# A hybrid decoder block on one core: where two plain weight loads of a paired projection stand in the load queue

## The chip, the cores and the metric

The kernel runs on one core of a Trainium2 chip. The metric is the device time of one execution in microseconds. Three runs of the kernel before gave 1426.63, 1428.28 and 1429.77 us; the median, 1428.28 us, is the time before. The engines are named as in the profile: PE is TensorE (PEld its weight loads), DVE VectorE, ACT ScalarE, POOL GpSimd, SP SyncE, which here only issues DMAs.

## The reference

One layer on x of shape (1, 256, 2048), float32: RMSNorm, one input projection for q, k, v and three gates, three causal token mixers, a gated merge, an output projection, then RMSNorm and a SwiGLU feed-forward layer of width 5632.

```python
h = rmsnorm(x, g_mix)
proj = h @ w_in                       # 2048 x 12288: q, k, v (16 heads of 128) and 3 gates of 2048
...
merged = (gates[:, :, 0] * (flat(o_a) @ w_branch[:ea])
          + gates[:, :, 1] * (flat(o_b) @ w_branch[ea:eb])
          + gates[:, :, 2] * (flat(o_c) @ w_branch[eb:]))
x = x + merged @ w_out
h2 = rmsnorm(x, g_ffn)
gu = h2 @ w_gu                        # 2048 x 11264: gate and up
x = x + (jax.nn.silu(gu[..., :D_FF]) * gu[..., D_FF:]) @ w_down
```

The attention mixers work on 256 tokens and are small beside the five weight matrices, which are read from HBM once each.

## The kernel before, in words

**Products.** Each float32 operand is split in two float32r parts, a high part (a cast on ACT) and a low part (source minus high part, on DVE): `split`, L109 and L110. A product of two operands is three matmuls (`product`, L162, matmuls at L164 to L166): high by high, low weight by high, high weight by low. A weight piece is 256 rows by 512 columns, 512 KB, in one tile of 128 x 2 x 512. `load` (L282) fetches one, `parts` (L288) splits one into w_hi and w_lo, which have five buffers each.

**Paired projections.** `project_pair` (L325) makes two column blocks A and B of 512 columns at once. Over the first two of the four 512-row chunks of the 2048 rows (`acts.wc`, chunks 0 and 1) it saves one product in eight: each chunk's weights are a 2 x 2 grid of pieces b11, b12, b21, b22 (first index the half of the rows, second the column block), and seven products of sums of pieces with sums of activations replace eight. They are called forms 1 to 7 here, each for both chunks. A `quarter` (L312) is the loading of one grid place for both chunks, two loads, into the pool `gx` under the name g_raw, which has six buffers. The other two chunks are done plainly: `rest` (L340) loads one piece under the name w_raw (four buffers, in `wpool`), splits it and makes twelve matmuls. Per pair there are eight loads of g_raw and eight of w_raw, 22 splits, and 84 + 96 matmuls of 512 columns.

**Banks.** X and Y take a pair of PSUM banks in turn (ps and qs); Z and V are z and v from the gate pairs on. The order of a pair is:

- `begin_pair` (L315), which the pair before runs ahead at its own end: loads b11, b12, splits b11, adds u = b11 + b12, loads b21 and splits it
- form 1 into X, a copy of X (`snapshot`, L303, L305), form 2 into Y, form 5 (with u) into Z, a copy of Z
- b22's two loads
- `rest` for the first two plain pieces of block B, into Z and V
- u += b22 (`add_into`, L308, L310) and form 6 into X, a third plain piece, b12 += b22 and form 7 into X, the fourth plain piece
- sums for the results c22 and c12, form 3 and form 4, four plain pieces of block A, the next pair's `begin_pair`

After it a gate pair scales and stores its results (L672, ACT), a gate/up pair does silu and the product with up (L889 on ACT, L890 on DVE).

**Order.** A scheduler orders the instructions of PE, DVE and ACT by a time model, but weight loads (except those of w_down and of the unpaired projections) are kept in program order on SP's queue by `fetch` (L105). So one queue carries, per pair, b11, b12, b21 (six g_raw), b22 (two g_raw), and the eight w_raw. A load waits on the queue until the buffer it takes has been read by its last readers; what is behind it on the queue waits too. With six buffers of g_raw, the two b22 loads take the buffers of b11, which are free once b11 is split.

**Which pairs there are.** Twenty: four for q and k, five for gates, and eleven for gate and up. In the q/k pairs Z and V are ps and qs too.

Of the kernel before, what the change touches and what calls it, by code (L numbers as in the profile page):

```python
# [57 lines left out]
def hybrid_block(ctx: ExitStack, tc: tile.TileContext, x, w_in, w_branch, w_out, w_gu, w_down, rel_bias, xT, gains,  # L58
# [24 lines left out]
    def pool(stack, name, side, bufs=1):  # L83
        return stack.enter_context(tc.tile_pool(name=name, bufs=bufs, side=side, reuse_waits="tile"))
# [8 lines left out]
    def half_kb(dt=F32):  # L93

        return scratch.tile([P, NB], dt, name="sc")
# [3 lines left out]
    def banks():  # L99

        turn.reverse()
        return [acc.tile([P, NB], F32, name=turn[1]) for _ in range(2)]
# [6 lines left out]
    def split(hi, lo, src, pin=False):  # L109
        for op in nc.scalar.copy(hi, src), nc.vector.tensor_sub(lo, src, hi.bitcast(F32)):  # L110
            if pin:
                tc.keep_in_program_order(op)
# [19 lines left out]
    def advance(queue):  # L132
        while queue:
            try:
                next(queue[0])
                return
            except StopIteration:
                queue.pop(0)
# [23 lines left out]
    def product(ps, ah, al, wh, wl, start=False, stop=False):  # L162
        how = dict(skip_group_check=True)
        nc.tensor.matmul(ps, ah, wh, start=start, stop=False, **how)  # L164
        nc.tensor.matmul(ps, ah, wl, start=False, stop=False, **how)  # L165
        nc.tensor.matmul(ps, al, wh, start=False, stop=stop, **how)  # L166
# [115 lines left out]
    def load(w, k, col0, pl=None):  # L282

        raw = pl.tile([P, 2, NB], F32, name="g_raw", bufs=6 if pl is gx else 4) if pl else wpool.tile([P, 2, NB], F32, name="w_raw", bufs=4)
        (nc.sync.dma_start if w is w_down else fetch)(raw, w[k * P:(k + 2) * P, col0:col0 + NB].rearrange("(k p) n -> p k n", p=P))
        return raw

    def parts(src):  # L288
        hi = wpool.tile([P, 2, NB], F32R, name="w_hi")
        lo = wpool.tile([P, 2, NB], F32R, name="w_lo")  # L290
        split(hi, lo, src)
        advance(stages)
        split_count[0] += 1
        if split_count[0] % 2:
            advance(slow_stages)
        for step in at_split.pop(split_count[0], ()):
            step()
        return hi, lo
# [4 lines left out]
    def snapshot(ps):  # L303
        sb = half_kb()
        nc.scalar.copy(sb, ps)  # L305
        return sb

    def add_into(dsts, srcs):  # L308
        for d, a in zip(dsts, srcs):
            tc.keep_in_program_order(nc.vector.tensor_add(d, d, a))  # L310

    def quarter(acts, w, kh, col0):  # L312
        return [load(w, 4 * c + 2 * kh, col0, gx) for c in acts.wc]

    def begin_pair(acts, w, colA, colB):  # L315

        b11, b12 = (quarter(acts, w, 0, col0) for col0 in (colA, colB))
        p11 = [parts(b) for b in b11]
        u = [gx.tile([P, 2, NB], F32, name="u") for _ in acts.wc]
        for a, b, d in zip(b11, b12, u):  # L320
            nc.vector.tensor_add(d, a, b)  # L321
        b21 = quarter(acts, w, 1, colA)
        return p11, b12, u, b21, [parts(b) for b in b21]

    def project_pair(acts, w, colA, colB, begun=None, nxt=None):  # L325

        cols = (colA, colB)
        X, Y = banks()  # L330
        Z, V = others()

        def form(ps, f, srcs, start, stop, split=False):
            for i, c in enumerate(acts.wc):
                wh, wl = srcs[i] if split else parts(srcs[i])
                for j in range(2):
                    product(ps, *acts.form(f, c, j), wh[:, j], wl[:, j], start and i + j == 0,
                            stop and i + j == len(acts.wc))

        def rest(n, k, p0, p1, start=False, stop=False):  # L340
            wh, wl = parts(load(w, k, cols[n]))
            for t, ps in ((1, p1), (0, p0)):
                for j in range(2):
                    product(ps, *acts.plain(t, k + j), wh[:, j], wl[:, j], bool(start and t == 1 and j == 0), stop and j == 1)

        ks = [k for c in range(KT // 4) if c not in acts.wc for k in (4 * c, 4 * c + 2)]
        p11, b12, u, b21, p21 = begun or begin_pair(acts, w, colA, colB)
        form(X, 1, p11, True, True, True)
        s1 = snapshot(X)
        form(Y, 2, p21, True, False, True)  # L350
        form(Z, 5, u, True, True)
        z5 = snapshot(Z)
        b22 = quarter(acts, w, 1, colB)
        rest(1, ks[0], Z, V, start=True)
        rest(1, ks[1], Z, V)
        add_into(u, b22)
        form(X, 6, u, False, True)
        x2 = snapshot(X)
        rest(1, ks[2], Z, V)
        add_into(b12, b22)  # L360
        form(X, 7, b12, False, True)
        x3 = snapshot(X)
        rest(1, ks[3], Z, V, stop=True)
        nc.vector.tensor_sub(z5, z5, x3)
        c22 = half_kb()
        nc.vector.tensor_add(c22, V, z5)
        form(Z, 3, b22, False, True)
        c12 = half_kb()
        nc.vector.tensor_sub(c12, Z, x2)
        for k in ks[:2]:  # L370
            rest(0, k, Y, X)
        add_into(u, b21)
        form(X, 4, u, False, False)
        for k in ks[2:]:
            rest(0, k, Y, X, stop=k == ks[-1])
        ahead = begin_pair(*nxt) if nxt else None
        c11 = half_kb()
        nc.vector.tensor_add(c11, Y, s1)
        return (c11, X, c12, c22), ahead
# [9 lines left out]
    p1 = pool(ph1, "p1", "left")  # L389
# [343 lines left out]
    for (kind, what), after in zip(units, units[1:] + [(None, None)]):  # L733
        if kind == "gates" and what[0] == chunks[4]:
            finish_stages(slow_stages)
            pat.close()
            acc2 = ctx.enter_context(tc.tile_pool(name="acc2", bufs=1, space=PSUM))
            others = beside
            o = Columns(pool(ph1, "o", "left"), "o", NH)
            for i in range(NH // 4):  # L740
                at_split[split_count[0] + 22 * i + 12] = [lambda k=4 * i: split_o(k)]
        nxt = pair_of(*after)
        if kind in ("qk", "gates"):
            ps, ahead = project_pair(*pair_of(kind, what), ahead, nxt)
            if others is in_turn:
                turn.reverse()
        else:
            ps = project(h, 0, w_in, 0, KT, V0 + what * NB if kind == "v" else gate_col(*what),
                         *((ps0, FIRST) if (kind, what) == ("v", 0) else ()))
            ahead = begin_pair(*nxt) if nxt else None  # L750
        finish_stages(stages)
        if kind == "v":
            keep_v(what, ps)
        elif kind == "qk":
            keep_qk(what, *ps)
        elif kind == "gate":
            keep_gate(*what, ps)
        else:
            keep_gate(*what[0], ps[:2])
            keep_gate(*what[1], ps[2:])  # L760
# [123 lines left out]
    for c in range(D_FF // NB):  # L884
        nxt = (h2, w_gu, (c + 1) * NB, D_FF + (c + 1) * NB) if c + 1 < D_FF // NB else None
        (g0, g1_, u0, u1), ahead = project_pair(h2, w_gu, c * NB, D_FF + c * NB, ahead, nxt)
        sg = [half_kb() for _ in range(NT)]
        for t, (g, u) in enumerate(((g0, u0), (g1_, u1))):
            nc.scalar.activation(sg[t], g, AF.Silu, scale=rstd2[:, t:t + 1])  # L889
            nc.vector.scalar_tensor_tensor(sg[t], u, rstd2[:, t:t + 1], sg[t], op0=ALU.mult, op1=ALU.mult)  # L890
        if c < NF // 4 - 2:
            to_a_by_dma(c, sg)
        else:
            stages.append(to_a(c, sg))
# [153 lines left out]
```

## Time and profile before

| | |
|---|---|
| median of three runs | 1428.28 us (1426.63 to 1429.77) |
| the profiled execution | 1427.54 us |
| its span, first to last instruction | 1425.8 us |
| DVE busy, ACT busy | 83%, 64% |
| DMA | 313.76 MB, mean 220 GB/s |
| w_raw loads from w_gu | 88, 512 KB each, 6.3 us from issue to landing (median) |
| g_raw loads from w_gu | 88, 512 KB each, 5.7 us (median) |

The page's first part gives busy time per engine and its share of the span. A group row reads: line, engine, operation, output <- inputs, count, then busy us, mean ns and the idle time of the engine before it with what ended it. In a timeline a row is start, length, engine, line, operation, and in brackets the idle time of that engine before it with its releaser. Rows of the same kind that follow each other are merged ("x2"). PE's matmuls overlap: each is shown with its full length, about 0.39 us, while one starts every 0.23 us, so what PE loses is read from the starts. In the chain of waits a row is start, length and what was under way.

### The profile page before, as it was taken

How to read it: one execution, taken by the hardware profiler on the slowest of the kernel's cores; microseconds unless marked ns; L12 is line 12 of the kernel's file. 1: busy time of each engine (PE TensorE's matmuls, PEld its weight loads, DVE VectorE, ACT ScalarE, POOL GpSimd, SP SyncE). 2: the span in 40 equal slices, each digit the busy share in tenths (PEclk: the TensorE clock that was granted, in tenths of full speed). 3: DMA queues.
4: the chain of work that ended last, by engine and by line, in shares of the span. 5: the costliest groups of instructions: out<-in, count | busy, mean ns of one | idle time of the engine just before them, and what ended most of it. 6: DMA issues, size and time to landing. Idle time of an engine off the chain costs nothing. (4 is left out here: it accounts for less than half of the span.)

```text
span 1425.8 us, 17593 instructions
## 1 busy us (share of the span) xinstructions
PE 1411.4 (99%) x6297; PEld 1159.1 (81%) x6297; DVE 1190.0 (83%) x1265; ACT 909.5 (64%) x1160; POOL 65.1 (5%) x121
## 2 busy tenths in 40 slices
PE   8999999999999999999999999999999999999998
PEld 6888788888888888888888887778888888788887
DVE  7898797867799997876689999999999998886775
ACT  7767777767666665444456677676777776654453
POOL 1000000000000002100100000000000010100000
PEclk9999999999999999999999999999999999999999
DMA  9764547374656757866686667577977786776552
GB/s 331 277 221 135 205 134 247 108 250 162 222 177 236 256 195 276 297 224 213 220 299 221 216 190 233 187 219 244 268 223 218 250 237 228 251 238 235 191 172 94
DMA packets 174056, 313.76 MB, mean 220 GB/s; under 512 B 29800, under 2 KB 32384, under 8 KB 173968
## 3 DMA queue, kind: packets, MB, share of 16 engines
q1 hardware_dynamic: 144672, 277.38, 58.0%
q0 software_dynamic: 8992, 29.45, 5.9%
q10 hardware_dynamic: 20304, 5.80, 2.8%
q8 instruction: 49, 0.80, 0.2%
q14 instruction: 39, 0.32, 0.1%
HBM read 293.17 MB, written 14.70 MB: 216 GB/s over the span
## 5 line engine op out<-in xcount | busy, mean ns | idle before, releaser
L110 DVE TENSOR_TENSOR w_lo<-w_raw,w_hi 128x1024 fp32r<-128x1024 f32 x332 | 403.3, 1221 | 122.4 <-ACT w_hi L110 119.4
L110 ACT CAST w_hi<-w_raw 128x1024 fp32r<-128x1024 f32 x332 | 346.3, 1050 | 171.4 <-PE qs L166 53.4
L110 ACT CAST w_hi<-g_raw 128x1024 fp32r<-128x1024 f32 x184 | 190.8, 1052 | 111.2 <-PE ps L166 31.9
L110 ACT CAST w_hi<-u 128x1024 fp32r<-128x1024 f32 x138 | 145.0, 1053 | 155.5 <-DVE u L310 77.5
L110 DVE TENSOR_TENSOR w_lo<-g_raw,w_hi 128x1024 fp32r<-128x1024 f32 x184 | 219.1, 1220 | 30.0 <-ACT w_hi L110 29.0
L110 DVE TENSOR_TENSOR w_lo<-u,w_hi 128x1024 fp32r<-128x1024 f32 x138 | 164.3, 1220 | 21.4 <-ACT w_hi L110 20.8
L165 PE MATMUL ps<-w_lo,h_hi 128*128 128x512 f32 x352 | 137.9, 392 | 1.2 <-DVE w_lo L110 1.2
L166 PE MATMUL ps<-w_hi,h_lo 128*128 128x512 f32 x352 | 137.3, 390 | 0.0
L164 PE MATMUL ps<-w_hi,h_hi 128*128 128x512 f32 x352 | 131.9, 391 | 0.0
L165 PE MATMUL qs<-w_lo,h_hi 128*128 128x512 f32 x332 | 129.7, 391 | 0.0
L166 PE MATMUL qs<-w_hi,h_lo 128*128 128x512 f32 x332 | 129.2, 390 | 0.0
L164 PE MATMUL qs<-w_hi,h_hi 128*128 128x512 f32 x332 | 122.9, 391 | 0.0
L310 DVE TENSOR_TENSOR u<-u,g_raw 128x1024 f32<-128x1024 f32 x80 | 94.1, 1218 | 0.0
L165 PEld LDWEIGHTS ps<-w_lo,h_hi 128*128 128x128 f32 x352 | 66.1, 188 | 15.5 <-DVE w_lo L110 1.9
L166 PEld LDWEIGHTS ps<-w_hi,h_lo 128*128 128x128 f32 x352 | 66.1, 188 | 13.6
L164 PEld LDWEIGHTS ps<-w_hi,h_hi 128*128 128x128 f32 x352 | 65.9, 188 | 13.3
L166 PEld LDWEIGHTS qs<-w_hi,h_lo 128*128 128x128 f32 x332 | 62.3, 188 | 12.8
L165 PEld LDWEIGHTS qs<-w_lo,h_hi 128*128 128x128 f32 x332 | 62.3, 188 | 12.8
L164 PEld LDWEIGHTS qs<-w_hi,h_hi 128*128 128x128 f32 x332 | 62.3, 188 | 12.7
L321 DVE TENSOR_TENSOR u<-g_raw 128x1024 f32<-128x1024 f32 x40 | 48.7, 1219 | 20.9 <-DMA g_raw<-in_w_in 16.3
L165 PE MATMUL v<-w_lo,h_hi 128*128 128x512 f32 x120 | 48.0, 400 | 2.9 <-DVE w_lo L110 2.7
L310 DVE TENSOR_TENSOR g_raw<-g_raw 128x1024 f32<-128x1024 f32 x40 | 47.1, 1219 | 0.0
(386 smaller groups left out, 2940.8 us busy)
## 6 DMA issues: line engine op xcount, KB each, us to landing
w_raw<-in_w_in SPq DMA_DIRECT2D x116, 512.0 KB, 5.0
g_raw<-in_w_gu SPq DMA_DIRECT2D x88, 512.0 KB, 5.7
w_raw<-in_w_gu SPq DMA_DIRECT2D x88, 512.0 KB, 6.3
g_raw<-in_w_in SPq DMA_DIRECT2D x72, 512.0 KB, 5.4
w_raw<-in_w_down SPq DMA_DIRECT2D x64, 512.0 KB, 4.7
w_raw<-in_w_branch SPq DMA_DIRECT2D x32, 512.0 KB, 5.9
w_raw<-in_w_out SPq DMA_DIRECT2D x32, 512.0 KB, 4.7
g_raw<-in_w_down SPq DMA_DIRECT2D x24, 512.0 KB, 5.3
```

The source lines that it names most:

```text
L110: for op in nc.scalar.copy(hi, src), nc.vector.tensor_sub(lo, src, hi.bitcast(F32)):
L164: nc.tensor.matmul(ps, ah, wh, start=start, stop=False, **how)
L165: nc.tensor.matmul(ps, ah, wl, start=False, stop=False, **how)
L166: nc.tensor.matmul(ps, al, wh, start=False, stop=stop, **how)
L310: tc.keep_in_program_order(nc.vector.tensor_add(d, d, a))
L321: nc.vector.tensor_add(d, a, b)
```

## The change

The first two plain loads of block B are issued before the two loads of b22 in program order, and so on the same queue; their splitting and products stay where they were.

```diff
-        def rest(n, k, p0, p1, start=False, stop=False):
-            wh, wl = parts(load(w, k, cols[n]))
+        def rest(n, k, p0, p1, start=False, stop=False, raw=None):
+            wh, wl = parts(raw or load(w, k, cols[n]))
...
         z5 = snapshot(Z)
+        first = [load(w, k, cols[1]) for k in ks[:2]]
         b22 = quarter(acts, w, 1, colB)
-        rest(1, ks[0], Z, V, start=True)
-        rest(1, ks[1], Z, V)
+        rest(1, ks[0], Z, V, start=True, raw=first[0])
+        rest(1, ks[1], Z, V, raw=first[1])
```

The queue of a pair then carries six g_raw, two w_raw, two g_raw, six w_raw. All twenty pairs run this code. The sizes, the buffers and the number of instructions of each kind stay the same.

## The prediction

> **What bounds the kernel now.** I read the page first, for the engine that carries the span.
>
> ```profile
> PE 1411.4 (99%) x6297; PEld 1159.1 (81%) x6297; DVE 1190.0 (83%) x1265; ACT 909.5 (64%) x1160; POOL 65.1 (5%) x121
> ...
> PEclk9999999999999999999999999999999999999999
> ```
>
> TensorE is busy nearly all the time at full clock, so only its small holes can be won. The next view groups who waited for whom, for the weight loads that run ahead of the matmuls, between 420 and 1080 us. That stretch holds most of the paired projections with their own banks z and v (gates and gate/up weights).
>
> ```profile
> PEld v L165 <- DVE w_lo L110: 6.8, 10, 1.1
> PEld qs L165 <- DVE w_lo L110: 2.0, 4, 0.8
> PEld ps L165 <- DVE w_lo L110: 2.0, 5, 0.5
> ```
>
> Columns: waiter, releaser, us in total, times, longest. Ten times the first product of a plain quarter into v waits for its low part, which VectorE makes from w_raw. To see why that is late I followed one of the ten, the pair around 940 us: the chain of waits, then the timelines of PE, ScalarE and VectorE.
>
> ```profile
> 940.02 6.07 DMA w_raw<-in_w_gu
> ```
>
> ```profile
> 947.73 0.39 PE L166 MATMUL z<-w_hi,h_slo 128*128 128x512 f32 x1
> 947.95 0.39 PE L164 MATMUL v<-w_hi,h_hi 128*128 128x512 f32 x1
> 948.53 0.50 PE L165 MATMUL v<-w_lo,h_hi 128*128 128x512 f32 x1 [0.19 <-DVE w_lo L110]
> 948.87 0.39 PE L166 MATMUL v<-w_hi,h_lo 128*128 128x512 f32 x1
> ```
>
> ```profile
> 940.44 2.19 ACT L110 CAST w_hi<-u 128x1024 fp32r<-128x1024 f32 x2 [2.12 <-PE qs L166]
> 942.54 0.72 ACT L889 ACTIVATE sc<-sc,rstd 128x512 f32<-128x512 f32 x1
> 943.16 0.67 ACT L889 ACTIVATE sc<-qs,rstd 128x512 f32<-128x512 f32 x1
> 943.73 0.57 ACT L305 COPY sc<-ps 128x512 f32<-128x512 f32 x1
> 946.17 1.05 ACT L110 CAST w_hi<-w_raw 128x1024 fp32r<-128x1024 f32 x1 [1.86 <-DMA w_raw<-in_w_gu]
> 947.12 1.35 ACT L860 COPY joined<-turned 128x1024 uint16<-128x1024 uint16 x1
> 948.35 1.03 ACT L110 CAST w_hi<-w_raw 128x1024 fp32r<-128x1024 f32 x1
> ```
>
> ```profile
> 923.42 1.22 DVE L110 TENSOR_TENSOR w_lo<-w_raw,w_hi 128x1024 fp32r<-128x1024 f32 x1
> 925.16 1.22 DVE L110 TENSOR_TENSOR w_lo<-w_raw,w_hi 128x1024 fp32r<-128x1024 f32 x1
> ...
> 937.17 4.63 DVE L110 TENSOR_TENSOR w_lo<-g_raw,w_hi 128x1024 fp32r<-128x1024 f32 x4
> 942.32 2.35 DVE L110 TENSOR_TENSOR w_lo<-u,w_hi 128x1024 fp32r<-128x1024 f32 x2
> 944.58 1.41 DVE L890 SCALAR_TENSOR_TENSOR sc<-sc,rstd 128x512 f32<-128x512 f32 x2
> 947.25 1.23 DVE L110 TENSOR_TENSOR w_lo<-w_raw,w_hi 128x1024 fp32r<-128x1024 f32 x1 [1.26 <-ACT w_hi L110]
> 949.42 1.23 DVE L110 TENSOR_TENSOR w_lo<-w_raw,w_hi 128x1024 fp32r<-128x1024 f32 x1 [0.94 <-ACT w_hi L110]
> 950.56 2.35 DVE L310 TENSOR_TENSOR u<-u,g_raw 128x1024 f32<-128x1024 f32 x2
> ```
>
> The load is issued at 940.02 and is in flight for 6.07 us, to 946.09; ScalarE stood idle 1.86 us for it; its cast ends at 947.22, VectorE's subtraction at 948.48, and PE goes on at 948.53. So in this pair the transfer ends last, and all else follows from its late issue. SyncE's own timeline, asked for at these moments, shows what kept it:
>
> ```profile
> 928.67 0.37 SPq L107 DMA_DIRECT2D g_raw<-in_w_gu  x1
> 938.42 0.37 SPq L107 DMA_DIRECT2D g_raw<-in_w_gu  x1
> 939.56 0.37 SPq L107 DMA_DIRECT2D g_raw<-in_w_gu  x1
> 940.02 0.42 SPq L107 DMA_DIRECT2D w_raw<-in_w_gu  x1
> ```
>
> 928.67 is the last b21 load. Then the queue stands until 938.42 and 939.56, when the first two of VectorE's four subtractions from 937.17 (1.14 us apart) have released the two b11 buffers that b22 takes. The plain loads, whose buffers were free, stand behind.
>
> **The change part by part.** No transfer, cast, subtraction or product is added or removed; two 512 KB loads per pair change places with two others on SyncE's queue. All twenty pairs get the new order.
>
> *When the plain loads go out.* w_raw has four buffers and each pair uses eight, so the first two loads of this pair take the buffers whose last readers are the subtractions at 923.42 and 925.16, over at 926.38. The last b21 load is issued at 928.67 and takes 0.37. The two plain loads can therefore go at about 929.1 and 929.6, eleven us sooner, and with the same 6.07 us land near 935.2, or some 2 us later if they queue behind b21. ScalarE asks for the first only at 942.6, when the two casts of u are over. The wait of 1.86 us goes entirely.
>
> *What b22 pays.* Its wait is for b11's buffers, as before, so it is still issued at 938.42 and 939.56, and its consumer, the addition at 950.56, keeps its cover. Two issues of 0.4 us fall into the ten us in which the queue stood: cost nothing. Without that cover (a first plain buffer free only after 938.42) b22 would be pushed by two transfers. In the bound that each takes the whole 6.07 us it lands by 952 and costs PE at most about 1.5 us in that pair; I take nothing, because the buffer was free twelve us before.
>
> *The instruction order.* The order of the changed program is known without running it. In seven pairs (three of the gates, four of gate/up) ScalarE's first cast of w_raw now stands ahead of the two activations and the copy of X (L889 and L305, in the gates four L672 and L305), and PE's first product into v some eleven products earlier, among the products of form 5. VectorE's first subtraction goes ahead of L890 in the gate/up pairs concerned. In the first gate/up pair small operations of the second norm change places too. Cost in this pair: the cast needs a w_hi buffer that form 1's second operand frees, and PE has done form 1's products at about 942.7. Here 24 products of forms 1 and 2 end at the first row below, so form 1 ended twelve steps of 0.23 us earlier:
>
> ```profile
> 945.46 0.39 PE L165 MATMUL z<-w_lo,h_shi 128*128 128x512 f32 x1
> ```
>
> The cast then runs from 942.7 to 943.8, the subtraction from 944.7 (after the two on u) to 945.9. PE wants the cast at 945.46 and the low part at 948.2: both in time by about 2 us. What moves behind, L889, L305 and L890, is at most 1.1 us later, and feeds a later stage: nothing. The second cast comes at about 946 and its subtraction ends near 948.5 instead of 950.65, where PE asks for it twelve products after the first, at about 948.2 + 12 x 0.23 = 950.9.
>
> In the gates four activations stand between the two casts, not two:
>
> ```profile
> 468.36 0.72 ACT L672 ACTIVATE sc<-sc,rstd 128x512 f32<-128x512 f32 x1
> 468.98 0.67 ACT L672 ACTIVATE sc<-ps,rstd 128x512 f32<-128x512 f32 x1
> 469.55 1.32 ACT L672 ACTIVATE sc<-sc,rstd 128x512 f32<-128x512 f32 x2
> ```
>
> That is 2.5 us and the copy's 0.5, so the second low part there comes about when it came before, and form 6 behind it as well, just in time for a PE that is half a us earlier.
>
> The waiting cast on ScalarE holds all behind it: after the 1.86 us at 946.17 the copy L860 starts only as the cast ends, at 947.12. [...]
>
> *The sum.* Between 947.95 and 948.87 PE made two steps in 0.92 us; undisturbed steps are 0.22 to 0.23 us (947.73 to 947.95), so the wait cost 0.46. The same wait stands in the weight loads' own row as 0.61 idle, so I take the idle time less 0.15 as loss. Ten waits of 6.8 us together: 6.8 - 10 x 0.15 = 5.3 us. The other two rows, 4.0 us in nine waits, are the form operands that VectorE makes after these:
>
> ```profile
> 959.58 0.39 PE L164 MATMUL ps<-w_hi,h_shi 128*128 128x512 f32 x1
> 960.07 0.50 PE L165 MATMUL ps<-w_lo,h_shi 128*128 128x512 f32 x1
> 960.40 0.40 PE L166 MATMUL ps<-w_hi,h_slo 128*128 128x512 f32 x1
> ```
>
> Here 0.82 us for two steps, 0.36 lost. In all 4.0 - 9 x 0.15 = 2.65 us. Where VectorE gets its second subtraction two us sooner and PE asks only half a us sooner, they go too; in the gates, and in the first gate/up pair (its one wait is the longest of the row, 0.8), they need not. Bounds 0 and 2.65; I take 1.0, a little under half. VectorE has room for it:
>
> ```profile
> 899.00:940.02 41.02, 40.16 (x175) 32.10 (x173) 37.76 (x38) 29.13 (x33) 0.00 (x0) 1.00 0.70 205
> 940.02:980.72 40.70, 40.41 (x176) 32.47 (x175) 38.20 (x37) 29.47 (x32) 1.43 (x2) 1.00 0.75 232
> 1104.00:1145.00 41.00, 41.00 (x182) 33.91 (x181) 38.60 (x37) 29.73 (x33) 1.43 (x2) 1.00 0.79 232
> ```
>
> (Stretch, its length, busy us of PE, weight loads, VectorE, ScalarE, POOL.) VectorE needs about 38 of 41 us per pair, and the last stretch shows PE busy throughout with the same VectorE load. The qk pairs give nothing: their waits lie outside these ten.
>
> Sum: 5.3 + 1.0 = 6.3 us. The profiled execution took 1427.54 us (span 1425.8 and 1.7 around it), 0.74 below the median of the three runs, 1428.28. So 1421.2 for such an execution and 1428.28 - 6.3 = 1422.0 for the median.
>
> **The rivals.**
>
> *The wait only moves.* VectorE is the next limit, 93% busy in a pair. If form 6's operand becomes what ends last, a pair keeps only part of the half us. For: the gates' reckoning above, and the waits at 960 that exist already. Against: 1104 to 1145, free of holes. With half of 5.3 us kept and nothing from form 6, 2.65 us: 1425.6.
>
> *The load was not held by the quarter, or is not needed sooner.* If the two plain loads still waited for a buffer, or ScalarE were late by itself, the time stays at 1428.3. For: the queue is one, and any wait in front of it holds them. Against: after 940.02 the first plain load goes out at once, and its buffer's last reader ended long before.
>
> *Slower: the cast that was moved forward waits.* If the first w_raw, or the w_hi buffer of form 1, comes late, ScalarE now stands before L889, L305 and the second cast, and PE at 945.46 before form 5 instead of after it. With today's landing at 946.09 the cast would end at 947.22 and PE lose 1.76 us where it loses 0.46: 1.3 us in each of seven pairs, 9.1 us, 1437.4. It decides from a cast that ends after 945.46, so a landing after 944.4. [...] Against: the issue at 929.1 leaves fifteen us for a transfer of six.
>
> **How the numbers follow.** Forecast 0.70, moved wait 0.17, no effect 0.05, slower 0.08. The forecast's own range runs from 5.3 + 2.65 = 7.95 us won (1420.3) to 4.0 (1424.3), if a quarter of the 5.3 comes back in the gates. To leave out no more than 2 in 10, the range takes in the moved wait with about 2 us to spare: 1420.0 to 1427.5. About 0.2%, 2.9 us, is what a measurement here can tell from none: faster means under 1425.4. The moved wait, at 1425.6, is shared between the two sides of that line, mostly to "within", and the forecast's upper edge loses a little: faster 0.73, within 0.19, slower 0.08.
>
> **What would show it.** In SyncE's timeline w_raw x2 stands between six and two g_raw, issued within a us after the last b21, landing before ScalarE's casts of u. ScalarE's waits for w_raw from w_gu all but vanish for these casts. The row of v waiting for w_lo falls from 6.8 us to under 1. If instead the qs and ps rows grow beyond 4.0 us, the wait moved; if a new row of v L164 waiting for ScalarE's w_hi appears with a us each, the slower rival holds. The prediction is wrong if the plain loads are issued late, or if the ten holes go and the span doesn't shrink.

## The result, and the profile after

The changed kernel takes 1418.45 us (median of five runs, 1418.05 to 1420.91) against 1428.54 for the kernel before on the same chip (median of five, too): a ratio of 0.9932, 95% interval 0.9917 to 0.9946, or 10.1 us. The profiled execution took 1418.35 us, its span is 1416.6 against 1425.8.

First part of the page of the changed kernel:

```profile
PE 1405.5 (99%) x6297; PEld 1160.9 (82%) x6297; DVE 1189.8 (84%) x1265; ACT 911.7 (64%) x1160; POOL 65.1 (5%) x121
```

The work is the same. PE's busy time fell by 5.9 us all the same, since part of a wait lies under the shown lengths of the matmuls around it (the one at 948.53 in the prediction is shown with 0.50 us, its neighbours with 0.39). The waits of the weight loads between 420 and 1080 us, changed kernel:

```profile
PEld ps L164 <- ACT w_hi L110: 1.5, 1, 1.5
```

That is the only row. The three rows of before, 10.8 us in 19 waits, are gone; one wait of 1.5 us is new.

SyncE's timeline at the last b21 load of the pair that was followed in the prediction, the plain load behind it, and the first b22 load:

```profile
920.42 0.37 SPq L107 DMA_DIRECT2D g_raw<-in_w_gu  x1
...
920.90 0.41 SPq L107 DMA_DIRECT2D w_raw<-in_w_gu  x1
...
930.17 0.37 SPq L107 DMA_DIRECT2D g_raw<-in_w_gu  x1
```

The first plain load goes 0.48 us behind b21 instead of 11.35. ScalarE's timeline in that pair (lines behind the inserted one carry a number higher by one, so L890 is the former L889):

```profile
933.94 2.19 ACT L110 CAST w_hi<-u 128x1024 fp32r<-128x1024 f32 x2 [1.46 <-PE qs L166]
936.44 1.06 ACT L110 CAST w_hi<-w_raw 128x1024 fp32r<-128x1024 f32 x1 [0.30 <-PE ps L166]
937.40 1.35 ACT L861 COPY joined<-turned 128x1024 uint16<-128x1024 uint16 x1
938.61 0.72 ACT L890 ACTIVATE sc<-sc,rstd 128x512 f32<-128x512 f32 x1
939.23 0.68 ACT L890 ACTIVATE sc<-qs,rstd 128x512 f32<-128x512 f32 x1
939.80 0.58 ACT L305 COPY sc<-ps 128x512 f32<-128x512 f32 x1
940.26 1.06 ACT L110 CAST w_hi<-w_raw 128x1024 fp32r<-128x1024 f32 x1
```

The cast waits 0.30 us for PE, for the w_hi buffer that form 1 frees, and no longer 1.86 for the transfer. PE in the same pair:

```profile
938.96 0.39 PE L164 MATMUL v<-w_hi,h_hi 128*128 128x512 f32 x1
...
941.45 0.39 PE L166 MATMUL z<-w_hi,h_slo 128*128 128x512 f32 x1
941.68 0.39 PE L165 MATMUL v<-w_lo,h_hi 128*128 128x512 f32 x1
941.90 0.39 PE L166 MATMUL v<-w_hi,h_lo 128*128 128x512 f32 x1
```

The first product into v stands ahead of the products of form 5, and the product with the low part follows them at 0.23 us, without a hole.

The new wait is a different thing. The chain of waits of the changed kernel around it:

```profile
919.29 10.63 DMA g_raw<-in_w_gu
929.92 0.02 issue
929.95 0.04 ACTq L110
929.98 0.04 issue
930.02 1.05 ACT w_hi L110
931.08 0.04 issue
931.12 0.50 PE ps L164
```

A b21 load took 10.63 us to land, where the median of the g_raw loads from w_gu is 6.2 in this profile, so the cast of b21 and PE's form 2 came late. The run e9 below asks whether that belongs to the change.

Where the time came from, read from the first or last start of one kind of instruction (views by tile; the row gives min/median/max length, first and last start). Before, then the changed kernel in its second profile (run e9):

```profile
L366 DVE TENSOR_TENSOR sc<-v,sc x15: 678/684/689, 413.5 to 1174.9; 128x512 f32<-128x512 f32 x15
...
L164 PE MATMUL qs<-w_hi,o_hi x64: 389/389/478, 543.8 to 630.6; 128*128 128x512 f32 x64
...
L164 PE MATMUL z<-w_hi,h_shi x88: 389/389/485, 735.9 to 1174.1; 128*128 128x512 f32 x88
```

```profile
L367 DVE TENSOR_TENSOR sc<-v,sc x15: 680/683/686, 412.9 to 1164.2; 128x512 f32<-128x512 f32 x15
...
L164 PE MATMUL qs<-w_hi,o_hi x64: 389/389/481, 541.3 to 627.5; 128*128 128x512 f32 x64
...
L164 PE MATMUL z<-w_hi,h_shi x88: 389/389/476, 732.7 to 1163.5; 128*128 128x512 f32 x88
```

| stretch | before | changed (e9) | gained |
|---|---|---|---|
| to the first result from v | 413.5 | 412.9 | 0.6 |
| on to the branch projection: gate pairs | 130.3 | 128.4 | 1.9 |
| branch and output projections | 192.1 | 191.4 | 0.7 |
| on to the last form in z: gate/up pairs | 438.2 | 430.8 | 7.4 |
| the rest, to the span's end (1425.8, 1415.7) | 251.7 | 252.2 | -0.5 |

### The profile page after: what moved, and what is told of

Same layout as the page of the kernel before. It is cut to its first block, busy times and chain, and to the rows that moved or that the text cites. A ratio compares the mean times of both kernels' runs of the same rounds, so it can differ in the third digit from the quotient of the medians.

```text
span 1416.6 us, 17612 instructions
## 1 busy us (share of the span) xinstructions
PE 1405.5 (99%) x6297; PEld 1160.9 (82%) x6297; DVE 1189.8 (84%) x1265; ACT 911.7 (64%) x1160; POOL 65.1 (5%) x121
## 4 chain that ended last, share of the span: by engine, by line
PE 89%; DVE 4%; DMA 3%; ACT 2%; issue 2%; SPq 0%; DVEq 0%; ACTq 0%
PE ps L165 10%; PE ps L164 10%; PE ps L166 10%; PE qs L165 10%; PE qs L166 10%; PE qs L164 10%; PE z L165 4%; PE z L166 4%; PE z L164 4%; PE v L165 3%; PE v L166 3%; PE v L164 3%; DVE w_lo L110 2%; PE tr L166 1%; PE tr L165 1%
## 5 line engine op out<-in xcount | busy, mean ns | idle before, releaser
L110 ACT CAST w_hi<-g_raw 128x1024 fp32r<-128x1024 f32 x184 | 191.4, 1052 | 120.5 <-PE ps L166 38.0
```

## The experiments

Each time is compared with that of the kernel before, measured beside it. Only one run of these ten, e9, is the changed kernel itself. The code cuts show what differs from the kernel before; where a cut leaves it out, `rest` takes the argument `raw` and uses the first two loads as in the change. Of the views of waits, the rows for w_lo and w_hi are shown.

**e1: half of the move.** The four loads alternate. PE's instruction order is that of the kernel before, so the queue is tried apart from the order on the engines.

```diff
-        b22 = quarter(acts, w, 1, colB)
-        rest(1, ks[0], Z, V, start=True)
-        rest(1, ks[1], Z, V)
+        b22, first = [], []
+        for c, k in zip(acts.wc, ks):
+            b22.append(load(w, 4 * c + 2, colB, gx))
+            first.append(load(w, k, cols[1]))
+        rest(1, ks[0], Z, V, start=True, raw=first[0])
+        rest(1, ks[1], Z, V, raw=first[1])
```

> The four loads in turn: b22 of chunk 0, plain 0, b22 of chunk 1, plain 1. PE's instruction order is that of the kernel before, ScalarE's differs in one place. Theory A (the holes come from the issue behind b22's wait alone): plain 0 is issued 1.2 us sooner and one transfer sooner in the queue, together about 2.5 us; the first products waited at most 1.1 us, so their waits go, and most of the gain of 10.1 us stays: 1418 to 1421, PEld v L165 waits for w_lo under 1 us of 6.8. Theory B (the gain comes from the new order on ScalarE, PE and VectorE): that order is not there, so 1426 to 1429.

1419.25 us, ratio 0.9938 (0.9920 to 0.9956). Waits of the weight loads, 420 to 1080 us:

```profile
PEld ps L165 <- DVE w_lo L110: 0.9, 2, 0.5
PEld qs L165 <- DVE w_lo L110: 0.8, 1, 0.8
```

No wait for v is left. So the place in the queue does nearly all of it, and the new order on ScalarE, PE and VectorE isn't what made the gain: theory B falls. (VectorE's order in e1 differs from that of before in seven places and ScalarE's in two, all about the second norm.) It also shows how shallow the lateness was. Counted from the issue of b22's first load, the first plain load lands 8.06 us later before, 4.97 later in e1, and 0.49 earlier in the first profile of the changed kernel (means of the eleven gate/up pairs): 3.1 us sooner do almost what 8.55 do.

**e2: one load in front.**

```diff
+        first = [load(w, ks[0], cols[1])]
         b22 = quarter(acts, w, 1, colB)
-        rest(1, ks[0], Z, V, start=True)
-        rest(1, ks[1], Z, V)
+        first.append(load(w, ks[1], cols[1]))
+        rest(1, ks[0], Z, V, start=True, raw=first[0])
+        rest(1, ks[1], Z, V, raw=first[1])
```

> Only the first plain load goes ahead of b22, the second stays right behind it. Theory A with the second load as cause of the form waits (PEld qs and ps L165, 4.0 us before): the second still comes one transfer sooner than before, lands near 946 in the pair of 940 us, and its split ends near 948.5: all waits go, 1418 to 1420. Theory C (form 6 and 7 wait for b22 itself, not for the splits): v waits gone, qs and ps waits stay near 3 to 4 us: 1421 to 1423.

1420.13 us, ratio 0.9942 (0.9924 to 0.9961). Same view:

```profile
PEld qs L165 <- DVE w_lo L110: 0.8, 1, 0.8
```

The v and ps waits are gone, with b22's loads still where they were: the form waits hung on the late splits, not on b22's landing. Theory C falls; the time is 0.1 above theory A's range. The one wait for w_lo left, 0.8 us, is that of the first gate/up pair. It stands in e1, e2, e4, e5 and e7 alike, and is gone in those where VectorE has the changed kernel's order of instructions throughout (e3, e9, e10), as in the first profile of the changed kernel. In e6, which has the old order of loads but another order of instructions, it is 0.2. So that 0.8 us seems to go with the order of the second norm's small operations rather than with the load's place; no run tried that alone.

**e3 and e4: only gate/up, only w_in.** The condition for e3; for e4 `w_in` stands in place of `w_gu`:

```diff
+        n_first = 2 if w is w_gu else 0
+        first = [load(w, k, cols[1]) for k in ks[:n_first]]
         b22 = quarter(acts, w, 1, colB)
+        first += [load(w, k, cols[1]) for k in ks[n_first:2]]
```

> The new load order for the eleven gate/up pairs alone, the nine pairs on w_in as before. From the drift between the two traces (9.2 us in all: 2.2 in the gates, 0.5 where the branch projection begins, 6.5 in gate/up): theory A says the stages add up and this one gives 6 to 7 us: 1421.5 to 1422.5. If the stages don't add up (a hole merely moves on), less than 5.

> The new load order for the nine pairs on w_in alone. By the same drift 2.2 to 3 us: 1425.5 to 1426.3, all of it in the five gate pairs, none in the four q/k pairs. If the half us at the start of the branch projection belongs to the gates' change, 2.7; if it is chance, 2.2.

e3: 1421.52 us, ratio 0.9952 (0.9934 to 0.9971); e4: 1425.75, ratio 0.9980 (0.9968 to 0.9993), before 1428.59. That is 7.1 and 2.8, together 9.9 of 10.1. The intervals leave each of the two open by about 2 us, but nothing says that a hole merely moved on. The stretch of the branch and output projections, 192.1 us before, takes 191.1 in e4 (542.7 to 733.8) and 192.4 in e3 (544.2 to 736.6), as if its gain went with the gates; but it takes 191.5 in e6 too, which has the old order of loads. So that 0.7 us is not shown to be the change's.

**e5 and e6: room instead of order.** The load order of before, and eight g_raw buffers, so that b22 needn't wait for b11's; e6 is only the smaller scratch pool that makes the room.

```diff
-    scratch = pool(ctx, "scratch", "right", 12)
+    scratch = pool(ctx, "scratch", "right", 8)
...
-        raw = pl.tile([P, 2, NB], F32, name="g_raw", bufs=6 if pl is gx else 4) if pl else ...
+        raw = pl.tile([P, 2, NB], F32, name="g_raw", bufs=8 if pl is gx else 4) if pl else ...
```

> The load order of the kernel before, but eight g_raw buffers instead of six, so that b22 never waits for the first quarter's room; to make room, the pool scratch has eight buffers instead of twelve (its cost is measured by the next run). Theory A (the wait for room holds the queue): the plain loads go out early by themselves, the waits PEld v, qs and ps for w_lo are under 1.5 us together instead of 10.8, and against the next run it is 8 to 10 us faster. If it is the position in the queue and not the wait: no gain against the next run.

> The kernel before with eight scratch buffers instead of twelve and nothing else: the reference for the run with eight g_raw buffers. No theory of the change bears on it; 1428 if the four buffers are spare, some us more if not.

e5: 1418.37 us, ratio 0.9930 (0.9918 to 0.9943); e6: 1427.96, ratio 0.9995 (0.9985 to 1.0005). Waits of e5 in the same view:

```profile
PEld qs L165 <- DVE w_lo L110: 0.8, 1, 0.8
```

SyncE's rows of the pair show that the wait for room is gone: the eight g_raw loads, b22's two the last of them, go out in 7.97 us in e5 and in 18.56 in e6.

```profile
915.19 7.97 SPq L107 DMA_DIRECT2D g_raw<-in_w_gu  x8
...
921.24 18.56 SPq L107 DMA_DIRECT2D g_raw<-in_w_gu  x8
```

With the old order of loads and no wait for room the gain is 9.6 us against e6. The scheduler orders some instructions differently in the two, but by e1 such an order isn't what gains. So it is the wait at the head of the queue that cost the time; order and room are two ways to take it away.

**e7: four in front.**

```diff
+        first = [load(w, k, cols[1]) for k in ks]
         b22 = quarter(acts, w, 1, colB)
...
-        rest(1, ks[2], Z, V)
+        rest(1, ks[2], Z, V, raw=first[2])
...
-        rest(1, ks[3], Z, V, stop=True)
+        rest(1, ks[3], Z, V, stop=True, raw=first[3])
```

> All four plain pieces of block B are loaded ahead of b22, not two. In the pair of 940 us the buffers of the third and fourth are free at 934.4 and 937.3, before b11's at 938.4. Theory A: b22 pays nothing that shows (two more transfers of 1.3 us before it, needed only at 950.6), and nothing more is won, since no wait is left there: 1417 to 1420. If b22 has less cover than the prediction said, waits of form 6 (qs, ps L165) come back: 1420 to 1424.

1418.80 us, ratio 0.9933 (0.9919 to 0.9946); the only wait for w_lo left is the 0.8 of the first gate/up pair. b22 has cover for two more transfers, and more than two loads in front win nothing.

**e8: the two plain loads exchanged.** Their place behind b22 stays; the one needed first comes second.

```diff
+        first = [load(w, k, cols[1]) for k in (ks[1], ks[0])][::-1]
```

> The order of the kernel before, with the first two plain loads in turn exchanged: the piece needed first comes one transfer (1.3 us) later than before. The scheduler orders some products differently for it. Theory A: in some fifteen pairs of gates and gate/up the hole grows by up to 1.3 us: plus 8 to 18 us, 1436 to 1446. If the landing isn't what ends last: within 2 us of 1428.5.

1449.56 us, ratio 1.0153 (1.0135 to 1.0171): 21.3 us slower. Waits of the weight loads, 420 to 1190 us:

```profile
PEld v L165 <- DVE w_lo L110: 11.9, 13, 1.1
PEld v L164 <- ACT w_hi L110: 7.6, 8, 2.4
PEld qs L165 <- DVE w_lo L110: 5.2, 8, 0.8
PEld ps L165 <- DVE w_lo L110: 4.7, 8, 0.8
```

The direction is theory A's, the size lies above its 8 to 18. In the eleven gate/up pairs the load that is needed first lands 1.3 us later than before, as meant (9.35 us behind the issue of b22's first load, against 8.06). That delay is paid twice: the product with the high part now waits too (7.6 us, a row that is 0.4 in the kernel before), and the form waits grow from 4.0 to 9.9 us. The scheduler also orders some products differently here, and what of the 21.3 us is due to that isn't known.

**e9: the changed kernel again.**

> The changed kernel once more, unchanged, for the hole of 1.4 us at 929.7 us that its first profile shows and the kernel before does not: there a b21 load took 10.6 us to land while the transposing DMAs held 16 engines from 920 to 926 us. If the hole belongs to the changed order, it is there again, in the same pair. If it is a chance meeting of a transpose and a load, it is gone or elsewhere, and the span is about 1.4 us shorter, 1415.2 (time 1416 to 1419).

1417.51 us, ratio 0.9927 (0.9911 to 0.9943); span 1415.7. The hole of 1.4 us is gone. ScalarE at the same place, where the first profile had a wait of 3.22 us for the load:

```profile
924.72 3.18 ACT L110 CAST w_hi<-g_raw 128x1024 fp32r<-128x1024 f32 x3
926.84 2.18 ACTq L853 DMA_TRANSPOSE turned<-sc  x1
929.33 1.06 ACT L110 CAST w_hi<-g_raw 128x1024 fp32r<-128x1024 f32 x1 [1.44 <-PE qs L166]
```

So the hole is no price of the change: the same program ran without it, and what stood beside it is told in the last section. The span is 0.9 us shorter, not 1.4: the part behind 1163 us took 0.6 longer than in the first profile.

**e10: room and order together**, the edits of the change and of e5.

> Both at once: eight g_raw buffers (scratch eight) and the changed load order. Theory A: the two remedies take away the same wait, so they don't add: 1416 to 1419, like either alone. If each removes holes of its own, 1410 to 1415.

1417.69 us, ratio 0.9927 (0.9911 to 0.9943), and no wait in that view at all. The remedies don't add. No version beats the changed kernel by more than the measurement tells.

## Why the prediction was right about the way and wrong about the size

Right, by its steps:

- *What bounds.* The transfer's late issue made the ten holes: e1 and e5 show it from two sides.
- *When the plain loads go out.* Foretold 0.4 to 0.5 us behind b21; it is 0.48. The transfer, taken as six us, took 13.04 in this pair in the first profile (landing at 933.94) and 6.10 in e9 (926.90). In the first profile the second load landed only at 935.18, during ScalarE's casts of u and not before them; so most of the fifteen us that the prediction counted as room were needed there: 2.2 us were left between the first landing and the end of those casts. ScalarE's nine waits for w_raw from w_gu, 12.5 us in the view of before, have no row after.
- *What b22 pays.* Nothing that shows, even with four loads in front (e7, 1418.80 us).
- *The instruction order.* The cast waits for form 1's buffer as reckoned, and for no transfer. What stands behind the cast starts as it ends or later: the cast runs from 936.44 to 937.50, L861 starts at 937.40, the two L890 at 938.61 and 939.23 and the copy of X at 939.80. That a waiting cast on ScalarE holds all behind it was read from the one row at 946.17; no run tries it alone. With the data there it costs 0.30 us on an engine that had the time, and the slower rival has no row.

Wrong was the sum: 6.3 us forecast, 10.1 measured, and the range ended at 1420.0. The terms, against waits before that fall into the two stretches of the table (the first of these fences is 413.5 to 543.8 us, the second 700 to 1175; view of the weight loads' waits, kernel before):

```profile
PEld v L165 <- DVE w_lo L110: 1.8, 3, 0.8
PEld qs L165 <- DVE w_lo L110: 0.3, 1, 0.3
PEld ps L165 <- DVE w_lo L110: 0.3, 1, 0.3
```

```profile
PEld v L165 <- DVE w_lo L110: 5.1, 7, 1.1
PEld ps L165 <- DVE w_lo L110: 1.7, 4, 0.5
PEld qs L165 <- DVE w_lo L110: 1.7, 3, 0.8
```

- *"Bounds 0 and 2.65; I take 1.0"* for the form waits. All went, so 1.65 too little. The reason given, that in the gates "the second low part there comes about when it came before", was wrong: the second cast had been held by its own landing, not by the four activations before it, so it too came sooner. In the gate pair around 432 us it waits for the transfer before, and follows the copy of X at once after:

```profile
432.23 1.05 ACT L110 CAST w_hi<-w_raw 128x1024 fp32r<-128x1024 f32 x1 [0.62 <-DMA w_raw<-in_w_in]
...
431.24 1.05 ACT L110 CAST w_hi<-w_raw 128x1024 fp32r<-128x1024 f32 x1
```

  The other doubt, the first gate/up pair, went with a changed order on VectorE (e2).
- *"The idle time less 0.15 as loss."* Idle time in these rows is 10.8 us in 19 waits (10.9 as rounded here). Read from the starts of the matmuls around each of them in the trace of before, PE lost 8.9 us there: the idle time less 0.10. I had read 0.15 from a single wait and two steps behind it. Such two steps hold 8.2 of the 8.9 over all the waits; the other 0.7 lies in some ten steps behind each, which take about 0.23 us where undisturbed ones take 0.227. In the pair followed, the fifteen steps between these two rows take 3.45 us, against 15 x 0.227 = 3.40:

```profile
948.87 0.39 PE L166 MATMUL v<-w_hi,h_lo 128*128 128x512 f32 x1
...
952.32 0.39 PE L165 MATMUL v<-w_lo,h_hi 128*128 128x512 f32 x1
```

  By the forecast's rule the 19 waits would give 7.95, so this term was 0.95 too small. Why the steps behind a wait are longer isn't shown.
- *Nothing was foreseen outside these rows.* The two stretches gained 1.9 + 7.4 = 9.3, which is 0.4 more than PE lost at these waits. The branch stretch gave 0.7, the start 0.6, the end took 0.5 back: 0.8 net. None of this is clear of the spread between profiles: with the old order of loads the gate/up stretch takes 438.2 us before, 437.9 in e4 and 437.1 in e6.

6.3 + 1.65 + 0.95 + 0.4 + 0.8 is 10.1, by which the span of e9 stands under that of before; the first two additions come from the rows and starts of these waits, the last two are what is left over. The range's lower end was the sum of what I had listed, 7.95 us, as if the reading of one wait and the list itself had no error. That is the step that put the measured time outside.

The rival "the wait only moves" had its chance from the same gates' reckoning; the rows it named, qs and ps, fell instead of growing.

## What to carry to other kernels

Here a load that waited for room held every load behind it on its queue (11.35 us from the last b21 load to the first plain one in the pair followed), also those whose buffers had long been free. Where such loads are needed first, put them in front or give the waiting one room: here either was worth 0.7%, and one transfer more of delay (a landing 1.3 us later), with some products reordered, cost 1.5% (e8). When several waits hang on one late transfer, count those further down the chain in full unless a row shows another cause for them, and read the loss per wait from many waits, with all the slower steps behind each, not from two steps behind one.

## What the runs showed of the hardware that I had not expected

Beside some transposing DMAs a load of 512 KB took twice as long: one b21 load 10.63 us in the changed kernel's first profile, the same load 5.18 in e9. Windows of the changed kernel's first profile, then of e9 (stretch, length, busy us of PE, PEld, DVE, ACT, POOL, clock, DMA share, GB/s):

```profile
920.00:925.00 5.00, 5.00 (x24) 4.14 (x23) 5.00 (x7) 4.92 (x7) 0.00 (x0) 1.00 1.31 138
...
920.00:925.00 5.00, 5.00 (x24) 4.14 (x23) 5.00 (x7) 4.92 (x7) 0.00 (x0) 1.00 1.10 366
```

In both a transpose had been issued shortly before on ScalarE's queue, at 916.71 and 916.61. The DMA queues from 920 to 926 us (q1 carries the loads, q10 the transpose: packets, MB, share of 16 engines' time), in the first profile, then in e9:

```profile
q10 hardware_dynamic: 1026, 0.26, 103.0%
q1 hardware_dynamic: 274, 0.52, 32.6%
...
q1 hardware_dynamic: 1022, 1.97, 89.0%
q10 hardware_dynamic: 1056, 0.26, 19.7%
```

The transpose moved the same 0.26 MB, but in the first the times of its packets add up to five times as much (103.0% against 19.7%; the share is that sum over the time of 16 engines), and the b21 load took 10.63 us; in the second that load took 5.18 and nothing was late there. It is not rare, nor does PE always wait for it: in e9 a transpose issued at 1000.0 took 16.6 us and the three loads issued next to it 10.7 to 14.5, without a wait of PE. With eight g_raw buffers (e5, e10) the median transpose took 11.0 and 11.1 us, in the other profiles 4.6 to 6.2. What slows the transpose's packets, and which of the two holds up the other, is not shown.
